# Attention block on one Trainium2 core: the output projection's rows 8 to 11 move from the last stage into the attention loop's fill

## The chip, the cores and the metric

The kernel runs on one NeuronCore of one Trainium2 chip. A core has five instruction streams that run side by side and wait for each other through semaphores: TensorE (PE, matrix products; its weight loads are shown as PEld), VectorE (DVE), ScalarE (ACT), GpSimd (POOL) and SyncE (SP), which only issues transfers between memory and the core. Each stream executes its instructions strictly in the order in which the program holds them. The metric is the device time of one execution in microseconds (us), lower is better; the median of several runs counts.

## What is computed

One layer on x of 2048 rows by 1024 columns. x is normalised and projected to q, k, v, a gate, and the two inputs of a recurrent branch. Eight heads of differential attention run causally over 2048 positions, and a gated linear recurrence runs beside them; both results, 1024 columns each, are concatenated and multiplied by w_out (2048 by 1024); the rows are normalised and added to x. Cut to its core:

```
qh = q.reshape(B, S, 8, 2, 64);  kh = k.reshape(B, S, 8, 2, 64);  vh = v.reshape(B, S, 8, 128)
o = diff_attention(qh, kh, vh, lam)        # softmax(q0 k0) v - lam * softmax(q1 k1) v, causal
y_attn = (rmsnorm(o, subln_g) * (1.0 - lam_init)).reshape(B, S, 1024) * silu(g_attn)
y_lru  = rg_lru(causal_depthwise_conv(x_lru, conv_w, conv_b), ...) * silu(g_lru)
y = jnp.concatenate([y_attn, y_lru], axis=-1) @ w_out
x = x + rmsnorm(y, post_norm_g)
```

All of it is float32. The kernel writes a float32 operand as a high part and a low part of a narrower type and forms each product from three matmuls (high by high, low by high, high by low).

## The kernel before

The sequence is cut into four chunks of 512 positions (j = 0 to 3) and sixteen rows of 128 positions ("row i" below is such a tile, i = 0 to 15). After the input projections, attention runs in two halves: half A takes the query pairs of chunks 0 and 1, half B those of chunks 2 and 3. This case is about half B and what follows it.

**A slot.** `attention` has one slot per unit: a unit is a head, a pair of query tiles (`pr`, 4 to 7 in half B), one of its two tiles and one of the two softmax maps, so half B has U = 128 units (0 to 127) and 12 slots more that only drain. In a slot the scores of the next unit are multiplied (`s`, four PSUM buffers), VectorE takes their maximum (`nm` is its negative, the last step of a unit), ScalarE takes the exponentials, VectorE combines the two maps into weights `p`, PE transposes them (`pw`), ScalarE and VectorE split them (`wh`, `wl`), and PE multiplies them by the values (`o`). Some slots after a chunk's last values a head's result is normalised in six steps, `norm1` to `norm6`: a square on ScalarE, a product with ones on PE (`pm`), an inverse square root on VectorE (`f`), its store and reload in another layout (`r_s`, then `rb`), a product on GpSimd (`yt`), and the store into `ya_s[j]`, from which the output projection reads. Rows 8 to 11 need `ya_s[2]` of all eight heads: the last head stores it at slot 129. Rows 12 to 15 need `ya_s[3]`, stored at slot 137.

**The fill.** Between these pieces stand matmuls of other work, drawn one by one from a generator. In half B it is `fill_out`, the output projection, in groups of 24 matmuls (8 blocks of 128 by three terms) for one row and one half of the output columns (`nh` 0 left, 1 right). The input side r = 1 is the recurrent branch, r = 0 attention. The groups are: r = 1 left and right for all 16 rows, r = 0 left and right for rows 0 to 7, and r = 0 right for row 8: 49 groups. A group loads its row's y (`yraw`, a single buffer, 512 KB), which GpSimd splits in four parts into `yh` and `yl` (two buffers) while the group ahead runs; its sum is in a single PSUM buffer `f`. For r = 0 VectorE adds the partial sum of r = 1 (`part`). When a row has both its halves, `finish` squares it on ScalarE (`junk`), multiplies by the norm's gain on GpSimd, forms the inverse square root on VectorE (`ss`), adds x (`xt`) and stores the output row.

**What sets the order.** The program hands out per slot a budget of fill matmuls (`FB` = 8.25, drawn as `owed`), and places scores, transposes, fill and values by a small clock of its own; the tile framework then orders each engine's stream by its own estimates, and adds the semaphores. SyncE's stream holds all transfers, and each waits there for its own condition with everything behind it.

**The last stage.** A pool of new buffers is opened on the left side of the memory. The remaining r = 0 products are the right halves of rows 9 to 15 and the left halves of rows 8 to 15 (`ps_y`, six PSUM buffers). The left weights (`w3h`, `w3l`) are loaded through SyncE and split on VectorE, three at a time between the right halves.

## Time and profile before

| what | value |
|---|---|
| median of 3 runs (lowest to highest) | 2247.93 us (2242.29 to 2249.29) |
| the profiled execution: its time | 2245.1 us |
| the profiled execution: span from the first to the last instruction | 2243.2 us |
| mean granted TensorE clock | 0.987 of full speed |
| busy share: PE, DVE, ACT, POOL | 96%, 67%, 45%, 36% |
| PE and DVE busy, 1720 to 1902 us (182 us of half B's loop) | 176.8 and 151.2 us |

Times in the views are counted from the span's start. A row of the table of stretches gives, for each engine, its busy time within the stretch and in brackets its instructions, then the granted clock, the busy share of the DMA engines and the bytes moved per second. A row of waits says which engine and line waited for which, in total, how often, and the longest. A row of the groups of instructions gives the count, busy time, mean duration in ns, and the idle time of that engine just before them with what ended most of it. A row of the chain of waits, which is followed back from the last instruction, gives start, duration and what ran or was awaited. "L1073" is line 1073 of the kernel.

### The profile page before, as it was taken

What the parts mean: (1) busy time and instruction counts of PE and PEld (TensorE: products, weight loads), DVE (VectorE), ACT (ScalarE), POOL (GpSimd) and SP (SyncE); (2) the same over time, 40 slices, a digit from 0 to 9 for tenths busy, and PEclk for the clock granted to TensorE, in tenths of its full rate; (3) what the DMA queues carried; (4) which work ended last, traced back from release to release, by engine and by line L of the source; (5) the groups of instructions that cost most, each with busy time, mean ns of one, the idle gap of its engine ahead of it and who ended that gap; (6) DMA issues with size and microseconds to landing.
All of it is one profiled execution on the core that took longest, in us unless ns stands there. A gap on an engine that the chain in (4) does not pass through costs nothing. (4 is left out here: it accounts for less than half of the span.)

```text
span 2243.2 us, 31726 instructions
## 1 busy us (share of the span) xinstructions
PE 2149.8 (96%) x11025; PEld 1786.9 (80%) x11025; DVE 1505.0 (67%) x3296; ACT 1003.3 (45%) x2259; POOL 803.1 (36%) x741
## 2 busy tenths in 40 slices
PE   7999999999899999999999998999999999999888
PEld 7888888888688888788888776888888887888666
DVE  6531144556677767777437776888888888889775
ACT  4211133444544444444225655665656656566211
POOL 1223044434411111111265653233533335345542
PEclk9999999999999999999999998999999999999999
DMA  6554332332478666665452207455464465654573
GB/s 214 151 155 150 103 102 78 97 104 77 117 195 218 165 172 169 175 168 133 132 182 70 67 33 178 117 150 143 124 177 127 124 168 140 169 160 142 161 230 131
DMA packets 346497, 317.93 MB, mean 142 GB/s; under 512 B 20257, under 2 KB 278370, under 8 KB 346338
## 3 DMA queue, kind: packets, MB, share of 16 engines
q1 hardware_dynamic: 346338, 315.91, 50.5%
q8 instruction: 87, 1.43, 0.3%
q14 instruction: 72, 0.59, 0.1%
HBM read 221.41 MB, written 94.44 MB: 141 GB/s over the span
## 5 line engine op out<-in xcount | busy, mean ns | idle before, releaser
L227 PE MATMUL ps<-hh,whi 128*128 128x512 f32 (+1 forms) x1456 | 563.7, 387 | 0.0
L227 PE MATMUL ps<-hh,wlo 128*128 128x512 f32 (+1 forms) x1456 | 562.9, 387 | 0.0
L227 PE MATMUL ps<-hl,whi 128*128 128x512 f32 (+1 forms) x1456 | 561.5, 386 | 0.0
L480 ACT ACTIVATE p<-s,nm 128x512 f32<-128x512 f32 (+3 forms) x640 | 392.6, 623 | 325.4 <-DVE nm L464 284.3
L199 POOL TENSOR_TENSOR wlo<-wraw,whi 128x1024 fp32r<-128x1024 f32 x88 | 221.8, 2521 | 526.4 <-DVE whi L198 173.4
L441 PE MATMUL s<-ks,qs 128*128 128x512 f32 (+2 forms) x1280 | 370.5, 387 | 19.3 <-ACT p L480 15.5
L227 PEld LDWEIGHTS ps<-hl,whi 128*128 128x128 f32 x1456 | 275.3, 189 | 51.7
L457 DVE TENSOR_REDUCE mx<-s 128x1 f32<-128x512 f32 x384 | 257.8, 684 | 87.4 <-PE s L441 86.1
L227 PEld LDWEIGHTS ps<-hh,wlo 128*128 128x128 f32 x1456 | 275.2, 189 | 51.5
L227 PEld LDWEIGHTS ps<-hh,whi 128*128 128x128 f32 x1456 | 275.3, 189 | 50.5
L441 PEld LDWEIGHTS s<-ks,qs 128*128 128x128 f32 x1280 | 213.2, 191 | 76.6 <-ACT p L480 46.6
L516 ACT ACTIVATE wh<-pw 128x512 fp32r<-128x512 f32 (+1 forms) x288 | 160.3, 577 | 158.5 <-PE pw L512 155.3
L70 POOL TENSOR_SCALAR yh<-yraw 128x256 fp32r<-128x256 f32 x196 | 92.6, 491 | 354.5 <-PE f L1073 303.4
L535 PE MATMUL o<-wh,vs 128*128 128x256 f32 (+1 forms) x1152 | 217.9, 280 | 0.2 <-ACT wh L516 0.2
L535 PEld LDWEIGHTS o<-wh,vs 128*128 128x128 f32 x1152 | 192.2, 190 | 17.0 <-ACT wh L516 1.0
L517 DVE TENSOR_TENSOR wl<-pw,wh 128x512 fp32r<-128x512 f32 (+1 forms) x288 | 185.7, 654 | 29.2 <-ACT wh L516 27.4
L498 DVE SCALAR_TENSOR_TENSOR p<-p,rr,p 128x128 f32<-128x128 f32 (+15 forms) x128 | 188.3, 1471 | 3.0
L512 PE MATMUL pw<-ident,p 128*128 128x128 f32 x1088 | 171.7, 273 | 9.9 <-DVE wl L517 5.7
L1073 PE MATMUL f<-woh,yh 128*128 128x512 f32 x392 | 162.3, 414 | 12.6 <-DVE yv L1089 4.6
L512 PEld LDWEIGHTS pw<-ident,p 128*128 128x128 f32 x1088 | 133.7, 140 | 43.6 <-issue 9.4
L535 PE MATMUL o<-wl,vs 128*128 128x256 f32 x576 | 162.8, 283 | 5.2 <-DVE wl L517 4.8
L71 POOL TENSOR_TENSOR yl<-yraw,yh 128x256 fp32r<-128x256 f32 x196 | 162.6, 850 | 0.1
(165 smaller groups left out, 3278.7 us busy)
## 6 DMA issues: line engine op xcount, KB each, us to landing
wraw<-in_w_in_dram SPq DMA_DIRECT2D x96, 512.0 KB, 4.3
qs<-q_s SPq DMA_DIRECT2D x128, 256.0 KB, 4.7
ks<-k_s SPq DMA_DIRECT2D x96, 256.0 KB, 5.6
vs<-v_s SPq DMA_DIRECT2D x48, 512.0 KB, 5.6
xt<-in_x_dram SPq DMA_DIRECT2D x32, 512.0 KB, 4.4
k_s<-hilo SPq DMA_DIRECT2D x64, 256.0 KB, 3.4
q_s<-hilo SPq DMA_DIRECT2D x64, 256.0 KB, 3.4
v_s<-hilo SPq DMA_DIRECT2D x32, 512.0 KB, 4.3
```

What stands on the lines that cost most here:

```text
L71: nc.gpsimd.tensor_tensor(out=lo, in0=src, in1=hi.bitcast(F32), op=ALU.subtract)
L199: nc.gpsimd.tensor_tensor(out=lo, in0=src, in1=hi.bitcast(F32), op=ALU.subtract)
L227: nc.tensor.matmul(out=ps[:, t0:t0 + n], lhsT=a[:, k, :], rhs=b[:, k, t0:t0 + n], start=(k == 0 and m == 0), stop=(k == KC - 1 and m == 2),)
L441: nc.tensor.matmul(out=ps[:, b0 - c0:b0 - c0 + nk], lhsT=qq[:, c, t * P:(t + 1) * P], rhs=kst[h, b0 // CH][:, c, 0:nk], start=(m == 0), st ...
L457: nc.vector.tensor_reduce(out=mx[:, pi:pi + 1], in_=s, axis=AX.X, op=ALU.max)
L480: nc.scalar.activation(out=p[:, c0:c1], in_=sc.pop((u, pi))[:, 0:c1 - c0], func=AF.Exp, bias=negm[u], accum_out=acc,)
L498: nc.vector.scalar_tensor_tensor(out=p0[:, 0:n], in0=p1[:, 0:n], scalar=rr[:, 1:2], in1=p0[:, 0:n], op0=ALU.mult, op1=ALU.add,)
L512: nc.tensor.transpose(pw[:, i * P:(i + 1) * P], wts[h, pr, t][:, kb * P:(kb + 1) * P], ident)
L516: nc.scalar.activation(out=wh[:, 0:n], in_=pw[:, 0:n], func=AF.Copy)
L517: nc.vector.tensor_tensor(out=wl[:, 0:n], in0=pw[:, 0:n], in1=wh[:, 0:n].bitcast(F32), op=ALU.subtract,)
L535: nc.tensor.matmul(out=po[h, j][:, oo:oo + w1 - w0], lhsT=a[:, kb % 4, :], rhs=w[:, w0:w1], start=(kb == 0 and m == 0), stop=(kb == 2 * pr ...
L1073: nc.tensor.matmul(out=ps, lhsT=a[:, k, :], rhs=b, start=(k == 0 and m == 0), stop=(k == 7 and m == 2),)
```

## The change

Five things change. First, r = 0 right for rows 9, 10 and 11 joins the fill, behind row 8: 52 groups. These four rows add the partial sum and store the result back over it (`part_s[1][i]`), and the last stage loads it from there. Second, the budget per slot is 9.4 up to slot 127 and 3 for the eight slots behind it; the fill of rows 8 to 11 may not be loaded before the last head has stored its chunk (`ya_done`), and until then the fill yields nothing, while its budget adds up. Third, in slots from U on, the budget is spent after the slot's transposes and values (this holds for half A as well). Fourth, the finished row of the fill (`yv`) gets a pool of its own with two buffers. Fifth, the last stage's pool moves to the right side, where the attention's buffers were; all eight left weights are loaded first, through ScalarE's queue, and split by ScalarE and VectorE; the order is the right halves of rows 12 to 15, then the left halves of 12, 8, 13, 9, 14, 10, 15, 11, each with its finish, and the loads of a row's y and sum stand ahead of it.

```diff
+    ya_done = set()
...
         def norm6(h, j):
             nc.sync.dma_start(out=ya_s[j][:, h, :], in_=nrm.pop((h, j))[1])
+            ya_done.add((h, j))
...
-            owed += per_slot(s)
-            nf = int(owed)
+            owed += per_slot(s) if s < U + 8 else 0
+            nf = int(owed) if s < U else 0
+            tail_fill = int(owed) if s >= U else 0
...
                     r = next(fill, "end")
                     if r == "end":
                         nf = 0
+                    elif r == "wait":
+                        nf = 0
...
+            for _ in range(tail_fill):
+                r = next(fill, "end")
+                if r in ("end", "wait"):
+                    break
+                owed -= 1
             run("C", combine)
...
-            gen = attention(range(4, 8), kv_p, pools, 4 * CH // SP, lambda s: FB if s > 1 else 6, 6, 5, 1)
+            gen = attention(range(4, 8), kv_p, pools, 4 * CH // SP, lambda s: (9.4 if s > 1 else 6) if s < 128 else 3, 6, 5, 1)
...
-        groups = [(r, nh, i) for r, nh in wsets for i in range((8, 16)[r])] + [(0, 1, 8)]
+        v_p = pb.enter_context(tc.tile_pool(name="rowB", bufs=2, side="right"))
+        groups = [(r, nh, i) for r, nh in wsets for i in range((8, 16)[r])] + [(0, 1, i) for i in range(8, 12)]
...
             for g, (r, nh, i) in enumerate(groups):
+                if ysp is None:
+                    while (H - 1, i // 4) not in ya_done:
+                        yield "wait"
+                    ysp, parts = load_y(r, i)
+                    for p in parts:
+                        split(*p)
...
-                if nxt:
+                ysp, parts = None, ()
+                if nxt and (nxt[0] or nxt[2] < 8 or (H - 1, nxt[2] // 4) in ya_done):
                     ysp, parts = load_y(*nxt[::2])
...
-                        yv = f_p.tile([P, D], F32, tag="yv", name="yv", bufs=1)
+                    if nh and i < 8:
+                        yv = v_p.tile([P, D], F32, tag="yv", name="yv")
...
-                    ends[i] = finish(f_p, i, yv, 1, 1, nc.gpsimd if i < FE else nc.vector)
-                    if i < 8:
-                        ends.pop(i)()
+                    finish(f_p, i, yv, 1, 1, nc.gpsimd)()
...
-                        nc.sync.dma_start(out=part_s[0][i][:, 0:CH], in_=st)
+                        nc.sync.dma_start(
+                            out=part_s[1][i][:, CH:] if i >= 8 else part_s[0][i][:, 0:CH], in_=st,
+                        )
...
-        y_p = p3.enter_context(tc.tile_pool(name="y", bufs=2))
+        y_p = p3.enter_context(tc.tile_pool(name="y", bufs=2, side="right"))
...
-            yh = y_p.tile([P, 8, P], F32R, tag="yh3", name="yh3", bufs=6)
+            yh = y_p.tile([P, 8, P], F32R, tag="yh3", name="yh3", bufs=5)
...
+        def load_w0(k):
+            raw = y_p.tile([P, CH], F32, tag="woraw3", name="woraw3", bufs=8)
+            nc.scalar.dma_start(out=raw, in_=w_out2[k * P:(k + 1) * P, 0:CH])
+            return raw
...
+            nc.scalar.activation(out=hi, in_=raw, func=AF.Copy)
+            nc.vector.tensor_tensor(out=lo, in0=raw, in1=hi.bitcast(F32), op=ALU.subtract)
...
         def left(i):
+            ends[i] = finish(y_p, i, yvs[i], 2, 1 + (i == 11), nc.gpsimd)
             ps = out_mm(i, w0)
...
-        load_ya(9)
-        load_ya(10)
-        for i in range(9, 12):
...
+        raws = [load_w0(k) for k in range(8)]
+        for k, raw in enumerate(raws):
+            split_w0(k, raw)
+        load_ya(12)
+        load_ya(13)
+        begin(12)
+        begin(13)
+        for i in range(12, 16):
+            if i < 14:
+                load_ya(i + 2)
+                begin(i + 2)
+            elif i == 14:
+                load_ya(8)
+                begin(8)
             right(i)
...
+        for i in range(8, 12):
+            left(i + 4)
+            if i < 11:
+                load_ya(i + 1)
+                begin(i + 1)
             left(i)
```

How the instructions move, at three places. **PE at the end of the loop:** the scores of the last unit (`s`), with the values (`o`) and transposes (`pw`) between them and what follows. Before:

```order
L441 MATMUL s<-ks,qs 128x512 x2
L535 MATMUL o<-wl,vs 128x256
L535 MATMUL o<-wh,vs 128x256
L441 MATMUL s<-ks,qs 128x512 x2
L535 MATMUL o<-wh,vs 128x256
L535 MATMUL o<-wl,vs 128x256
L557 MATMUL pm<-ones_235,sq 128x2 x4
L1073 MATMUL f<-wol_20001,yh 128x512
L1073 MATMUL f<-woh_20011,yh 128x512
L1073 MATMUL f<-woh_20011,yl 128x512
L1073 MATMUL f<-wol_20012,yh 128x512
L1073 MATMUL f<-woh_20070,yh 128x512
```

Now (the product with ones, `pm`, is the norm of the last head's chunk 2; it stood behind the last scores before):

```order
L559 MATMUL pm<-ones_235,sq 128x2 x4
L537 MATMUL o<-wl,vs 128x256
L443 MATMUL s<-ks,qs 128x512 x2
L537 MATMUL o<-wh,vs 128x256
L514 MATMUL pw<-ident,p_20689 128x128
L443 MATMUL s<-ks,qs 128x512 x2
L514 MATMUL pw<-ident,p_20834 128x128
L443 MATMUL s<-ks,qs 128x512 x2
L514 MATMUL pw<-ident,p_20689 128x128
L514 MATMUL pw<-ident,p_20834 128x128
L443 MATMUL s<-ks,qs 128x512 x2
L514 MATMUL pw<-ident,p_20689 128x128
```

The fill (`f`) that followed the last scores is gone there; none stands between the scores of unit 124 and the place that follows, and all groups up to 47 stand ahead of unit 124's.

**PE in the drain, now:** the last transposes, the first matmuls of group 48 (row 8) and a value between them:

```order
L537 MATMUL o<-wl,vs 128x256
L514 MATMUL pw<-ident,p_20967 128x128
L514 MATMUL pw<-ident,p_21069 128x128
L514 MATMUL pw<-ident,p_20967 128x128
L514 MATMUL pw<-ident,p_21069 128x128
L514 MATMUL pw<-ident,p_20967 128x128
L514 MATMUL pw<-ident,p_21069 128x128 x2
L1087 MATMUL f<-woh_19208,yh 128x512
L537 MATMUL o<-wh,vs 128x256
L1087 MATMUL f<-woh_19208,yl 128x512
L1087 MATMUL f<-wol_19209,yh 128x512
L1087 MATMUL f<-woh_19217,yh 128x512
```

Group 48 begins behind the last transposes; one row of the last values stands behind its first matmul, the others behind its last.

**SyncE in the drain, now:** the transfers of the last head's norm (`r_s`, `rb`, `ya_s`), of groups 48 to 51 (`yraw` the load of y, `part` the sum to be added, `fo` the result) and of row 12 (the last row here). The first piece ends with the load for group 51:

```order
L572 DMA r_s_2_194<-f_21135 128x4
L576 DMA rb<-r_s_2_194 128x512
L585 DMA ya_s_198<-yt 128x512
L992 DMA yraw<-ya_s_198 128x8x128 x2
L1109 DMA part_s_8_220<-fo 128x512
L992 DMA yraw<-ya_s_198 128x8x128
L1083 DMA part<-part_s_9_221 128x512
L992 DMA yraw<-ya_s_198 128x8x128
```

and it goes on:

```order
L1109 DMA part_s_9_221<-fo 128x512
L1083 DMA part<-part_s_10_222 128x512
L1109 DMA part_s_10_222<-fo 128x512
L572 DMA r_s_3_195<-f_21471 128x4
L1083 DMA part<-part_s_11_223 128x512
L576 DMA rb<-r_s_3_195 128x512
L585 DMA ya_s_199<-yt 128x512
L1109 DMA part_s_11_223<-fo 128x512
L1130 DMA yraw_21595<-ya_s_199 128x8x128
```

Before, the loads of rows 9 to 11 for the last stage stood between the norm of chunk 3 and row 12's load; now groups 49 to 51 are loaded ahead of that norm's `r_s`, and row 12's load stands behind the store of group 51's result.

More of the change, by code (lines that the diff above doesn't have):

```diff
@@ L1058, in fill_out @@
                 c0 = nh * CH
-                if i >= 8 and r == 0:
-                    yv = f_p.tile([P, D], F32, tag="yv", name="yv", bufs=1)
-                    nc.sync.dma_start(out=yv, in_=part_s[1][i])
-                    part = yv[:, CH:]
-                    ys[i], yvs[i] = ysp, yv
-                elif r == 0:
-                    if nh:
-                        yv = f_p.tile([P, D], F32, tag="yv", name="yv", bufs=1)
+                if r == 0:
+                    if nh and i < 8:
+                        yv = v_p.tile([P, D], F32, tag="yv", name="yv")
                         nc.sync.dma_start(out=yv[:, 0:CH], in_=part_s[0][i][:, 0:CH])
@@ L1085, in fill_out @@
                             raw_wo(*nxt[:2], k + 4)
-                    if k % 2 and nxt:
+                    if k % 2 and parts:
                         split(*parts[k // 2])
-                if r == 0 and nh == 1:
+                if r == 0 and nh == 1 and i < 8:
                     nc.vector.tensor_tensor(out=yv[:, CH:], in0=ps, in1=part, op=ALU.add)
-                    ends[i] = finish(f_p, i, yv, 1, 1, nc.gpsimd if i < FE else nc.vector)
-                    if i < 8:
-                        ends.pop(i)()
+                    finish(f_p, i, yv, 1, 1, nc.gpsimd)()
                 else:
@@ L1116, in load_ya @@
             nc.sync.dma_start(out=raw, in_=ya_s[i // 4][:, :, (i % 4) * P:(i % 4 + 1) * P])
-            yh = y_p.tile([P, 8, P], F32R, tag="yh3", name="yh3", bufs=6)
-            yl = y_p.tile([P, 8, P], F32R, tag="yl3", name="yl3", bufs=6)
+            yh = y_p.tile([P, 8, P], F32R, tag="yh3", name="yh3", bufs=5)
+            yl = y_p.tile([P, 8, P], F32R, tag="yl3", name="yl3", bufs=5)
             split3(yh, yl, raw, SY)
@@ L1134, in hymba_kernel, with split_w0, begin, right @@
         w0 = []
-        def right(i):
+        def load_w0(k):
+            raw = y_p.tile([P, CH], F32, tag="woraw3", name="woraw3", bufs=8)
+            nc.scalar.dma_start(out=raw, in_=w_out2[k * P:(k + 1) * P, 0:CH])
+            return raw
+        def split_w0(k, raw):
+            hi = y_p.tile([P, CH], F32R, name=f"w3h{k}", bufs=1)
+            lo = y_p.tile([P, CH], F32R, name=f"w3l{k}", bufs=1)
+            nc.scalar.activation(out=hi, in_=raw, func=AF.Copy)
+            nc.vector.tensor_tensor(out=lo, in0=raw, in1=hi.bitcast(F32), op=ALU.subtract)
+            w0.append((hi, lo))
+        def begin(i):
             yvs[i] = y_p.tile([P, D], F32, tag="yv3", name="yv3", bufs=5)
             nc.sync.dma_start(out=yvs[i], in_=part_s[1][i])
+        def right(i):
             ps = out_mm(i, w1)
             nc.vector.tensor_tensor(out=yvs[i][:, CH:], in0=ps, in1=yvs[i][:, CH:], op=ALU.add)
-            ends[i] = finish(y_p, i, yvs[i], 2, 1 + (i == 15), nc.vector if FY else nc.gpsimd)
         def left(i):
+            ends[i] = finish(y_p, i, yvs[i], 2, 1 + (i == 11), nc.gpsimd)
             ps = out_mm(i, w0)
@@ L1146, in left @@
             ends.pop(i)()
-        load_ya(9)
-        load_ya(10)
-        for i in range(9, 12):
-            for k in ((0, 1, 2), (3, 4, 5), (6, 7))[i - 9]:
-                raw = y_p.tile([P, CH], F32, tag="woraw3", name="woraw3")
-                nc.sync.dma_start(out=raw, in_=w_out2[k * P:(k + 1) * P, 0:CH])
-                hi = y_p.tile([P, CH], F32R, name=f"w3h{k}", bufs=1)
-                lo = y_p.tile([P, CH], F32R, name=f"w3l{k}", bufs=1)
-                split3(hi, lo, raw, SW)
-                w0.append((hi, lo))
-            right(i)
-            load_ya(i + 2)
-        for i in range(8, 16):
+        raws = [load_w0(k) for k in range(8)]
[12 more added lines that the diff above has]
+                begin(8)
+            right(i)
+        for i in range(8, 12):
[3 more added lines that the diff above has]
+                begin(i + 1)
             left(i)
-            if i < 12:
-                right(i + 4)
-                if i + 6 < 16:
-                    load_ya(i + 6)
     pf.close()
```

## The prediction

> **What bounds the kernel now.** First the page, then a table of the last stretches, then what TensorE (PE) waited for in them.
>
> ```profile
> span 2243.2 us, 31726 instructions
> PE 2149.8 (96%) x11025; PEld 1786.9 (80%) x11025; DVE 1505.0 (67%) x3296; ACT 1003.3 (45%) x2259; POOL 803.1 (36%) x741
> ```
>
> PE is the bound by share, so only its idle time can be won or lost: the change moves matmuls and adds none. Where that idle time lies, by stretches (us, then busy us of each engine):
>
> ```profile
> core 0: us, PE busy (x) PEld busy (x) DVE busy (x) ACT busy (x) POOL busy (x), PEclk, DMA share, GB/s
> 1946.00:2060.00 114.00, 111.44 (x652) 94.22 (x651) 100.74 (x240) 71.57 (x195) 60.23 (x71) 1.00 0.51 143
> 2060.00:2081.00 21.00, 20.14 (x117) 17.20 (x117) 20.29 (x48) 12.21 (x34) 8.06 (x10) 1.00 0.32 100
> 2081.00:2112.00 31.00, 26.28 (x170) 22.43 (x168) 22.73 (x53) 11.64 (x28) 18.58 (x24) 0.99 0.51 154
> 2112.00:2172.00 60.00, 46.18 (x169) 35.22 (x170) 43.24 (x73) 7.24 (x20) 32.55 (x29) 0.89 0.75 241
> 2172.00:2234.50 62.50, 62.45 (x264) 50.25 (x262) 36.67 (x92) 7.96 (x22) 17.71 (x12) 0.97 0.42 144
> 2234.50:2243.20 8.70, 0.00 (x0) 0.00 (x0) 4.14 (x13) 0.72 (x2) 1.26 (x1) 0.70 0.30 121
> ```
>
> In the score loop PE is nearly full, but in its last 21 us VectorE (DVE) is just as full (20.29). The drain (2081 to 2112) and the hand-over to the last stage (2112 to 2172) hold 18.5 us of idle PE, at a lowered clock. The maxima of the last scores, which end the loop:
>
> ```profile
> L464 DVE TENSOR_REDUCE nm<-mx x4: 142/151/157, 2059.9 to 2080.8; 128x1 f32<-128x4 f32 x4
> ```
>
> So unit 124's maximum stands at 2060 and unit 127's, the last (call it T), at 2081. From 2060 to the end PE waited most for:
>
> ```profile
> PE f L1073 <- DVE yv L1089: 4.6, 1, 4.6
> PE ps_y L1128 <- DVE yh L202: 4.5, 1, 4.5
> PE f L1073 <- DVE f L563: 1.9, 1, 1.9
> ```
>
> The first is a row's finish blocking VectorE, the second is row 12's load behind other loads. Both places are rewritten.
>
> **The loop, denser.** By the order of instructions 1019 fill matmuls stood ahead of unit 124's last score, now 1152: 133 more. The chain of waits and the waits of the loop (1374 to 2060) price them:
>
> ```profile
> 2070.40 1.16 PE f L1073 x5
> ...
> PE s L441 <- ACT p L480: 11.0, 16, 1.9
> ```
>
> 1.16/5 is 0.232 us each: 133 are +30.9 us. Against it, waits of scores for ScalarE's exponentials (11.0 us in 16 pieces) can be filled by work that stands between; bounds 0 and -11, I take -3, because the scores stay where a free buffer puts them and few of the waits have fill left in their slot.
>
> All eight row finishes now fall into the loop; before, most fell into its end and the drain. One finish on VectorE:
>
> ```profile
> L1006 DVE SCALAR_TENSOR_TENSOR xt<-yv,ss,xt 128x1024 f32<-128x1024 f32 x5 | 6.4, 1281 | 2.3 <-DMA xt<-in_x_dram 2.1
> L96 DVE TENSOR_SCALAR ss<-ss 128x1 f32<-128x1 f32 x15 | 4.0, 266 | 0.2
> L97 DVE SCALAR_TENSOR_TENSOR ss<-ss 128x1 f32<-128x1 f32 x15 | 2.6, 171 | 0.1
> L1002 DVE TENSOR_TENSOR ss<-ss 128x1 f32<-128x1 f32 x5 | 1.3, 260 | 4.6 <-ACT junk L995 4.6
> L89 DVE TENSOR_SCALAR ss<-ss 128x1 int32<-128x1 int32 x5 | 0.8, 154 | 0.1
> ```
>
> 1.28 + 3 x 0.27 + 3 x 0.17 + 0.26 + three small ones of about 0.15 are 3.3 us. In 1946 to 2060 stood two chains and one xt; by the new order of VectorE seven finishes stand ahead of unit 124's end. That is 5 x 3.3 + 1.3 = 17.8 more, so 118.5 us of VectorE; at the 97% that it reached in the next row (20.29 of 21) it needs 122.4. PE with 13 more matmuls there needs 111.44 + 3.0 + its 2.6 of idle = 117. The stretch turns to VectorE: +5 (0 if the second row buffer smooths it, +10 if every finish stalls VectorE by its 1.4 us of idle, 4.6 and 2.1 over five). Unit 124: 2060 + 30.9 - 3 + 5 = 2092.9.
>
> **The end of the loop, empty.** Between units 124 and 127 there is no fill now (about 32 matmuls in the old order). VectorE there:
>
> ```profile
> L1006 DVE SCALAR_TENSOR_TENSOR xt<-yv,ss,xt 128x1024 f32<-128x1024 f32 x2 | 2.6, 1278 | 0.0
> L96 DVE TENSOR_SCALAR ss<-ss 128x1 f32<-128x1 f32 x4 | 1.0, 259 | 0.0
> L97 DVE SCALAR_TENSOR_TENSOR ss<-ss 128x1 f32<-128x1 f32 x4 | 0.6, 146 | 0.0
> ```
>
> These and one add (0.7) leave, 4.9, and one finish (3.3) stays: 18.7 of VectorE, at 97% 19 us instead of 21. PE's 20.14 - 7.4 does not bind. T = 2112.
>
> **Group 48 waits for row 8.** Its y comes from the last head's norm, which ends in slot 129; what ran there before was rows 4 to 7, whose y had long been there. The links (chain of waits; times to landing; the loads from issue to landing):
>
> ```profile
> 2087.52 2.56 DMA r_s<-f
> ...
> 2090.16 6.14 DMA rb<-r_s
> ...
> 2096.44 2.63 POOL yt L580
> ...
> DMA to landing us min/median/max: 3.5/4.1/6.1
> ...
> ya_s<-yt SPq DMA_DIRECT2D x4, 256.0 KB, 2.0
> r_s<-f SPq DMA_DIRECT2D x3, 2.0 KB, 2.1
> part<-part_s SPq DMA_DIRECT2D x9, 256.0 KB, 4.2
> ...
> DMA to landing us min/median/max: 4.0/4.8/7.6
> ...
> L580 POOL TENSOR_TENSOR yt<-yt,rb x16: 1521/1549/2641, 1458.4 to 2127.9; 128x512 f32<-128x512 f32 x16
> ```
>
> The first landing row is rb's, the second yraw's. In the new order the reciprocal root stands right behind T with nothing but one other instruction: 3.5 us (6.5 before: T to 2087.5). Then r_s 2.1, rb 4.1, the product 1.6, the store 2.0, yraw 4.8 and gaps: yraw lands at T + 18.3 (25 at the times of the chain above, 15.5 at the minima). Call this L: 2130. PE has only transposes and values until then; after them it stands at group 48's first matmul, with the last 24 values behind that.
>
> **Four groups on one raw buffer.** GpSimd splits each y in four parts:
>
> ```profile
> 2099.04 0.78 POOL L70 TENSOR_SCALAR yh<-yraw 128x256 fp32r<-128x256 f32 x2
> 2099.77 1.44 POOL L71 TENSOR_TENSOR yl<-yraw,yh 128x256 fp32r<-128x256 f32 x2
> ```
>
> Twice this, 4.35 us, and only then the single raw buffer takes the next row: 4.35 + 4.8 = 9.1 per group, while its matmuls need 24 x 0.232 = 5.6. In the loop a group lasted 2.6 slots and hid it; here the load is bare. Group 51's y is split at L + 32. Worse is SyncE's order: group 51's load waits there for the split of group 50 (L + 22.6); behind it stand the store of group 49, part of row 10 (4.2, so L + 27.5), the store of group 50 and only then r_s of rows 12 to 15 at about L + 28.2.
>
> **Row 12.** From there the same links: 2.1 + 4.1 + 1.6 + 2.0 + 4.8 and, for the last stage's split:
>
> ```profile
> 2147.87 6.90 DMA yraw<-ya_s
> ...
> 2154.79 0.69 DVE yh L202
> ...
> L203 POOL TENSOR_TENSOR yl<-yraw,yh 128x1024 fp32r<-128x1024 f32 x5 | 12.3, 2468 | 9.9 <-DVE yh L202 9.9
> ...
> 2171.69 62.78 PE ps_y L1128 x264
> ```
>
> 0.7 + 2.5, with gaps 18.3: row 12 runs from L + 46.5 (40 at minima, 53 at the slow times). Before, the right halves of rows 9 to 11 covered this; now PE is idle from about L + 33. Then 288 matmuls without a stop at 62.78/264 = 0.238: 68.5, and after so long a gap a slow start:
>
> ```profile
> 2132.24 0.76 PE L1073 MATMUL f<-woh,yh 128*128 128x512 f32 x1 [4.59 <-DVE yv L1089]
> ...
> 2135.67 0.40 PE L1073 MATMUL f<-wol,yh 128*128 128x512 f32 x1
> ```
>
> Eight matmuls took 3.4 us instead of 1.9, so +1. The end after the last matmul stays 8.7 (last row of the table).
>
> **The left weights.** Eight loads on ScalarE's queue stand behind its last square, about L + 23; their split is done long before left needs it at L + 69. What leaves is PE's wait for these weights in the hand-over, one part of its idle 18.5 us, already out of my sum. Their 2.1 MB meet group 51's load and rb; at the 241 GB/s of the table they are 8.7 us of traffic. I take 0, since group 51 is not what row 12 waits for; bound +4.
> The Trainium skill (DMA: Bandwidth & Descriptors, Issuing engines are not separate DMA queues) says that transfers started by ScalarE and SyncE run on the same 16 engines and interleave, so that another queue saves issue time alone. By that rule the +4 is the likelier end, and the sum would be 2259 instead of 2255; no run here has a second queue.
>
> **The rest.** The first half's drain is reordered too (fill behind transposes), but its fill has two accumulators and no load to wait for: 0, bounds -2 and +2. The second row buffer, the other side of the memory and five instead of six split buffers are in the terms above or free of PE.
>
> **Sum:** 2130 + 46.5 + 68.5 + 1 + 8.7 = 2254.7 of span; the profiled execution took 2245.1, 1.9 over its span, so 2256.6, say 2257, +0.5%. The median of the runs is 2.8 above the profiled one, within their spread.
>
> **Rivals.** *The loop swallows the fill* (faster): all 11 us of score waits are filled, VectorE keeps up (no +5), and links run at their minima. Unit 124 2079.9, T 2099, L 2114.5, end 2114.5 + 40 + 78.2 = 2232.7, time 2235. For it: PE has those waits and the drain's DMA engines are quieter than before. Against: VectorE's 20.29 of 21. *Loop free, drain as forecast* (no change): -5 and 0 in place of -3 and +5: 2247.7, time 2250. For it: yv waits disappear with two buffers. *Collisions in the drain* (slower still): rb, yraw and part run at the times of the chain while the left weights load; L at T + 22, row 12 at L + 53: 2265, time 2267. It decides once rb takes 6 us instead of 4.1. *The fill is not moved as said*: the order rules it out; only its wait for row 8 can differ.
>
> **How the numbers follow.** Forecast 0.49 (its own range 2250 to 2264), swallowed 0.18, loop free 0.20, collisions 0.13. About 0.3% (7 us) is the least that a measurement of this kernel tells from no change: from 2241 to 2255. Faster 0.18; same: loop free and the low end of the forecast, 0.27; slower 0.55. Range 2237 to 2269.
>
> **What would show it.** Right: no fill between units 124 and 127, that stretch at 18 to 20 us; unit 124 near 2093; a PE gap ahead of group 48 released by GpSimd's yh or yl; groups 48 to 51 about 9 us apart, each released by GpSimd; a gap of 10 us or more ahead of the first last-stage matmul, released by VectorE's cast or GpSimd's yl behind yraw; then 288 matmuls without a gap. Wrong: unit 124 before 2083, group 48 within 12 us of T, or row 12 within 5 us of group 51's end.

## The result and the profile after

The changed kernel takes 2268.61 us (median of 4 runs, 2266.16 to 2271.08), the kernel before, run beside it, 2245.47. The ratio is 1.0102, with a 95% interval of 1.0078 to 1.0126: slower by 1.0%. Forecast were 2257 us (+0.5%), within 2237 to 2269. The profiled execution of the changed kernel took 2271.1 us, 1.8 over its span.

First the head of the page, then the table of stretches, cut at the places that the prediction named (columns as before).

```profile
span 2269.3 us, 31770 instructions
PE 2153.8 (95%) x11025; PEld 1793.3 (79%) x11025; DVE 1491.8 (66%) x3287; ACT 1006.0 (44%) x2267; POOL 803.5 (35%) x768
```

```profile
1968.00:2095.30 127.30, 117.26 (x669) 95.77 (x667) 120.38 (x300) 74.59 (x211) 55.24 (x67) 1.00 0.57 166
2095.30:2115.40 20.10, 15.24 (x85) 12.22 (x85) 18.62 (x46) 12.02 (x31) 0.67 (x1) 0.92 0.06 26
2115.40:2131.20 15.80, 12.33 (x75) 10.74 (x74) 9.31 (x23) 7.60 (x17) 1.97 (x3) 0.78 0.25 68
2131.20:2164.00 32.80, 25.17 (x109) 20.22 (x110) 8.00 (x17) 0.73 (x2) 16.69 (x31) 0.90 0.29 89
2164.00:2182.20 18.20, 6.97 (x22) 4.92 (x21) 1.39 (x2) 0.00 (x0) 3.88 (x2) 0.69 0.67 185
2182.20:2257.00 74.80, 68.54 (x287) 55.68 (x287) 51.16 (x95) 14.45 (x38) 33.53 (x21) 0.93 0.61 200
2257.00:2269.30 12.30, 0.00 (x0) 0.00 (x0) 7.73 (x22) 0.86 (x4) 3.34 (x3) 0.50 0.39 136
```

PE's work is the same 11025 matmuls. Its idle time lies in the loop's end, in the drain, and behind the last matmul. The maxima of units 124 to 127 in the view of one tile, which give unit 124 at 2095.3 and T at 2115.4:

```profile
L466 DVE TENSOR_REDUCE nm<-mx x4: 142/148/155, 2095.2 to 2115.3; 128x1 f32<-128x4 f32 x4
```

**Groups 48 to 51.** From PE's timeline, the first matmuls of groups 48, 49 and 50, the last of the values (`o`) that stand between them, and the last matmul of group 50; in brackets the idle time ahead and what ended it.

```profile
2131.23 0.51 PE L1087 MATMUL f<-woh,yh 128*128 128x512 f32 x1 [0.59 <-POOL yh L70]
...
2139.67 0.50 PE L1087 MATMUL f<-woh,yh 128*128 128x512 f32 x1 [0.94 <-POOL yh L70]
...
2149.24 0.47 PE L1087 MATMUL f<-woh,yh 128*128 128x512 f32 x1 [2.06 <-DVE fo L1108]
...
2154.04 0.28 PE L537 MATMUL o<-wl,vs 128*128 128x128 f32 x1
...
2157.89 0.40 PE L1087 MATMUL f<-wol,yh 128*128 128x512 f32 x1
```

The groups start 8.4 and 9.6 us apart, then 12.7 (group 51 at 2161.89). The last value of the last head is multiplied only at 2154.04, behind groups 48 and 49 and half of 50. Until then ScalarE cannot square that head (2154.41), and the norm of rows 12 to 15 cannot begin. Its inverse square root on VectorE (timeline; first, slowest and last step) ends at 2161.8:

```profile
2156.58 0.16 DVE L565 SCALAR_TENSOR_TENSOR f<-pm,f 128x4 f32<-128x4 f32 x1 [0.79 <-PE pm L559]
...
2157.44 0.68 DVE L81 SCALAR_TENSOR_TENSOR f<-f 128x4 f32<-128x4 f32 x1
...
2161.66 0.15 DVE L82 SCALAR_TENSOR_TENSOR f<-f 128x4 f32<-128x4 f32 x1
```

SyncE issues its store `r_s` 0.3 us behind that end, right behind the store of group 50's result (`part_s`, SyncE's timeline):

```profile
2152.11 0.53 SPq L992 DMA_DIRECT2D yraw<-ya_s  x1
...
2161.77 0.32 SPq L1109 DMA_DIRECT2D part_s<-fo  x1
2162.14 0.42 SPq L572 DMA_DIRECT2D r_s<-f  x1
...
2165.68 0.32 SPq L576 DMA_DIRECT2D rb<-r_s  x1
2170.75 0.32 SPq L585 DMA_DIRECT2D ya_s<-yt  x1
```

So the root came last here, but SyncE's queue was close behind it. The addition of group 50's result (`fo`, 0.7 us) stands in the middle of the root. Without the root, that result could have been stored at about 2159, and `r_s` could have followed at about 2159.4, 2.7 us earlier than it did (an estimate from the end of group 50's last matmul and these durations).

PE's waits from 2060 on have row 12's load at their head. Group 51 waits behind the same root, because the addition that empties the sum buffer (`fo` of group 50) stands in it:

```profile
PE ps_y L1142 <- DVE yh L202: 9.5, 1, 9.5
...
PE f L1087 <- DVE f L82: 3.6, 1, 3.6
```

**The last stage.** The chain of waits (start, duration, what ran) passes from PE to VectorE in its middle and never returns:

```profile
2172.81 5.88 DMA yraw<-ya_s
...
2182.17 30.50 PE ps_y L1142 x119
2212.70 0.70 DVE yv L1173
...
2214.18 2.37 DVE ss L1013
...
2220.85 0.70 DVE yv L1173
...
2229.18 0.61 DVE yv L1173
...
2237.24 0.70 DVE yv L1173
...
2243.27 0.61 DVE yv L1173
```

Only 119 of the 288 matmuls are on the chain. From the first left halves on, each row's addition waits for VectorE's finish of the row ahead: 8.2 us apart three times, then 5.9. A row's 24 matmuls need 24 x 0.238 = 5.7. PE is never held up, since six PSUM buffers stand between, but it is done by 2250.7 and the finishes run on to 2269.3: 18.6 us behind the last matmul instead of 8.7. The 8.2 has its reason in the second kind of row, `ss` L1013: an addition of 128x1 that takes 2.37 us there, and 0.16 in the last five rows. GpSimd's timeline stands beside it:

```profile
2214.12 2.40 POOL L203 TENSOR_TENSOR yl<-yraw,yh 128x1024 fp32r<-128x1024 f32 x1 [11.97 <-DVE yh L202]
```

The addition starts 0.06 us behind the split and ends with it. The same pair stands once in the kernel before, where the alternating order kept it off the path (VectorE's and GpSimd's timelines):

```profile
2186.19 2.40 DVE L1002 TENSOR_TENSOR ss<-ss 128x1 f32<-128x1 f32 x1 [0.25 <-ACT junk L995]
```

```profile
2186.17 2.41 POOL L203 TENSOR_TENSOR yl<-yraw,yh 128x1024 fp32r<-128x1024 f32 x1 [3.20 <-DVE yh L202]
```

The 5.9 us of the later rows hold more of the same kind. The change also moved the first half of a finish, the square and the product of the right half, from the right half's place to the left half's, so that two products of GpSimd (2.55 us) now stand beside VectorE's root where one (1.30 us) stood before. The second of the root's steps with two inputs (L97) lasts until GpSimd's second product ends (VectorE's timelines; a late row of the changed kernel, then one of the kernel before):

```profile
2240.47 0.91 DVE L97 SCALAR_TENSOR_TENSOR ss<-ss 128x1 f32<-128x1 f32 x1
```

```profile
2226.61 0.16 DVE L97 SCALAR_TENSOR_TENSOR ss<-ss 128x1 f32<-128x1 f32 x1
```

In the kernel before, the last four left halves follow each other too, without a right half or a split between them, but 5.56 us apart, and VectorE waits 0.27 us for PE ahead of each of the last three: there PE set the pace. No run moves the second product back alone, so its share is not tested.

### The profile page after: what moved, and what is told of

Read it like the earlier page. It is cut to its first block, busy times and chain, and to the rows that moved or that the text cites. A ratio compares the mean times of both kernels' runs of the same rounds, so it can differ in the third digit from the quotient of the medians.

```text
span 2269.3 us, 31770 instructions
## 1 busy us (share of the span) xinstructions
PE 2153.8 (95%) x11025; PEld 1793.3 (79%) x11025; DVE 1491.8 (66%) x3287; ACT 1006.0 (44%) x2267; POOL 803.5 (35%) x768
## 3 DMA queue, kind: packets, MB, share of 16 engines
q10 hardware_dynamic: 1152, 2.10, 0.3%
## 5 line engine op out<-in xcount | busy, mean ns | idle before, releaser
L443 PE MATMUL s<-ks,qs 128*128 128x512 f32 (+2 forms) x1280 | 365.7, 386 | 25.6 <-ACT p L482 22.4
L70 POOL TENSOR_SCALAR yh<-yraw 128x256 fp32r<-128x256 f32 x208 | 99.4, 496 | 370.9 <-PE f L1087 327.0
L1087 PE MATMUL f<-woh,yh 128*128 128x512 f32 x416 | 170.0, 409 | 14.5 <-ACT fo L1113 6.9
L1087 PE MATMUL f<-woh,yl 128*128 128x512 f32 x416 | 169.8, 408 | 1.0 <-POOL yl L71 1.0
L1087 PE MATMUL f<-wol,yh 128*128 128x512 f32 x416 | 169.0, 406 | 0.0
```

The source lines that it names most:

```text
L70: nc.gpsimd.tensor_scalar(out=hi, in0=src, scalar1=1.0, scalar2=1.0, op0=ALU.mult, op1=ALU.mult)
L443: nc.tensor.matmul(out=ps[:, b0 - c0:b0 - c0 + nk], lhsT=qq[:, c, t * P:(t + 1) * P], rhs=kst[h, b0 // CH][:, c, 0:nk], start=(m == 0), st ...
L1087: nc.tensor.matmul(out=ps, lhsT=a[:, k, :], rhs=b, start=(k == 0 and m == 0), stop=(k == 7 and m == 2),)
```

## The experiments

Ratios are to the kernel before, run beside each on the same chip; the changed kernel has 1.0102. "Alternating" is the last stage in the order right 12, left 8, right 13, left 9, right 14, left 10, right 15, left 11, and then the left halves of 12 to 15, as follows (the last row's finish is halved at row 15 instead of 11):

```diff
         load_ya(12)
-        load_ya(13)
+        load_ya(8)
         begin(12)
-        begin(13)
-        for i in range(12, 16):
...
+        begin(8)
+        for k in range(4):
+            right(12 + k)
+            if k < 3:
+                load_ya(13 + k)
+                begin(13 + k)
+            left(8 + k)
+            if k < 3:
+                load_ya(9 + k)
+                begin(9 + k)
+        for i in range(12, 16):
+            left(i)
```

### The budget back at 8.25

```diff
-lambda s: (9.4 if s > 1 else 6) if s < 128 else 3
+lambda s: (8.25 if s > 1 else 6) if s < 128 else 3
```

> The changed kernel with the old budget of 8.25 fill matmuls per slot in place of 9.4; all else as changed. Theory (the drain is bound by one raw buffer, 9.1 us per group, and by the wait for row 8): about 109 matmuls move from the loop into the drain, so the last score maximum comes 25 to 30 us earlier (about 2088), but groups 44 to 51 then go through the single raw buffer one after another, 8 x 9 us, and the time stays within 2256 to 2268 (2268.6 now). Rival (the denser loop itself, where VectorE cannot follow, is what was lost): the drain stays as long as now from the last score on, and the time falls to 2240 to 2250.

Measured: 2264.74, ratio 1.0073 [1.0054, 1.0092]. T is back at 2085.3, but 192 matmuls of fill now stand behind T instead of 96, with five row finishes among them, and PE waits there (waits of 2085 to 2200):

```profile
PE f L1087 <- POOL yh L70: 10.6, 2, 6.8
PE f L1087 <- DVE fo L1108: 9.1, 2, 6.5
```

The time hardly falls: what is taken out of the loop is paid again behind it. How much of the loss lies in the loop with 9.4 shows only beside 8.75, below.

### One finished-row buffer, and the pool on the other side

```diff
-        v_p = pb.enter_context(tc.tile_pool(name="rowB", bufs=2, side="right"))
+        v_p = pb.enter_context(tc.tile_pool(name="rowB", bufs=1, side="right"))
```

> The changed kernel with one buffer instead of two for the fill's finished row. Theory: the second buffer bought little, because the loop is bound by VectorE's work and not by waits for the row: 2266 to 2271. Rival (two buffers kept VectorE from stalling in every finish, 1.4 us each): 2274 to 2282.

Measured: 2266.67, ratio 1.0075 [1.0049, 1.01]; the interval overlaps that of the changed kernel. The second row buffer carries nothing that can be measured here.

```diff
-        y_p = p3.enter_context(tc.tile_pool(name="y", bufs=2, side="right"))
+        y_p = p3.enter_context(tc.tile_pool(name="y", bufs=2))
```

> The changed kernel with the last stage's pool on the left side of the memory, as before the change. Theory (on the right the left weights' buffers lie where the attention's last product lay, so ScalarE's loads start only when that product is stored and collide with row 12's load): the eight loads start about 18 us earlier, next to ScalarE's last square, row 12's load lands in 4.8 instead of 5.9 us and the sums of the last stage in 4 to 5 instead of 7.7: time 2265 to 2268. Rival (the collision holds up the whole last stage): 2255 to 2262.

Measured: 2267.51, ratio 1.0087 [1.0065, 1.0109], no difference. The expectation that the eight loads of the left weights would start 18 us earlier failed: ScalarE's queue issues them at 2170.91 here and, in the changed kernel, at

```profile
2172.92 10.85 ACTq L1152 DMA_DIRECT2D woraw<-in_w_out_dram  x8
```

ScalarE's last instruction ahead of them is the square at 2154.41. In both runs the loads go out 2.2 us behind the issue of the last chunk's store (`ya_s`, 2168.72 here and 2170.75 there; it lands 2.0 us after its issue) and 0.1 us behind row 12's own load. With the budget 8.75 alone (below) the store is issued at 2129.59 and the loads at 2131.83, again 2.2 us later, but 4.3 us ahead of row 12's load. So they go with that store, as the expectation said, but on either side of the memory. Why they wait for it on the left side too was not found.

### The alternating last stage

The diff is the one above.

> The changed kernel with another order of the last stage: right 12, left 8, right 13, left 9, right 14, left 10, right 15, left 11, then left 12 to 15, instead of all right halves first. Theory (left halves in a row are bound by VectorE's finish, 5.9 to 8.2 us each against 5.6 us of matmuls): rows finish during the right halves, the stretch from the first last-stage matmul to the end falls from 87 us to 78 to 82 (up to 3 us may be lost on left weights that come late), time 2260 to 2264. Rival (the last stage is slow because of the lowered clock after the gap ahead of it): no change, 2267 to 2270.

Measured: 2260.69, ratio 1.0053 [1.0033, 1.0073], about 8 to 11 us less than the changed kernel. In the profiles 6 us of this lie in the last stage: from row 12's first running matmul to the end it takes 81 us instead of 87. The rest lies ahead of it, where the two kernels are alike: T is 2110.6 in this profile, 2115.4 in that of the changed kernel, and between 2110.6 and 2117.8 in all runs with 9.4. With a right half between two left halves VectorE has 11.2 us for a finish, and PE sets the pace; only the last four left halves, with nothing between them, are 5.95 us apart again. The 2.4 us addition still occurs, once:

```profile
L1013 DVE TENSOR_TENSOR ss<-ss x8: 145/160/2401, 2193.5 to 2248.6; 128x1 f32<-128x1 f32 x8
```

### Two raw buffers for the fill's y

With one finished-row buffer, since the memory does not hold both.

```diff
-YR = 1
+YR = 2
...
-        v_p = pb.enter_context(tc.tile_pool(name="rowB", bufs=2, side="right"))
+        v_p = pb.enter_context(tc.tile_pool(name="rowB", bufs=1, side="right"))
```

> The changed kernel with two raw buffers for the fill's y (and one buffer instead of two for the finished row, which alone made no difference). Theory (groups 48 to 51 are paced by load, then split, 8.5 us each, and SyncE holds r_s of rows 12 to 15 behind the load for group 51): the groups follow each other in 6 to 7 us, row 12 starts 38 to 43 us after group 48 instead of 48, time 2257 to 2261. Rival (their pace is set by the partial sums and the single sum buffer, and row 12's chain by its own links): no change, 2265 to 2269.

Measured: 2264.48, ratio 1.0068 [1.0044, 1.0091], some 2 us less than with one raw buffer (the run with one finished-row buffer, 1.0075), which the intervals do not tell apart. The groups do run closer. Row 12's first matmul stands 41.6 us behind group 48's, as the theory had it, against 46.5 in the run with one raw buffer and one row buffer and 48.4 in the changed kernel. The time did not follow by as much: T is 1.7 us later in this profile than in that run's, and the gap ahead of row 12, 9.5 us in the changed kernel and 11.5 in that run, is now (waits from 2090 on)

```profile
PE ps_y L1142 <- DVE yh L202: 12.7, 1, 12.7
```

The load for group 51 no longer holds anything: SyncE has issued it by 2142.1, and `r_s` goes out at 2156.9, within 0.4 us of its root's end and again right behind the store of group 50. The root's chain begins with the last values, and here too they stand behind groups 48 and 49: ScalarE squares the last head at 2151.7. GpSimd is idle during the root now, and this takes 2.6 us instead of 5.2 (4.1 with one raw buffer and one row buffer):

```profile
2153.92 0.16 DVE L565 SCALAR_TENSOR_TENSOR f<-pm,f 128x4 f32<-128x4 f32 x1 [0.80 <-PE pm L559]
...
2156.41 0.15 DVE L82 SCALAR_TENSOR_TENSOR f<-f 128x4 f32<-128x4 f32 x1
```

Two raw buffers, one row buffer and the alternating last stage together:

> Two raw buffers (with one buffer for the finished row) and the alternating last stage together, budget 9.4 as changed. Theory: the two gains add up, 8 and 9 us: 2249 to 2254. Rival (row 12's own chain ends at the same time whatever the groups do): 2259 to 2262, as with the alternating order alone.

Measured: 2254.61, ratio 1.0031 [1.0013, 1.005], just over the theory's range and well under the rival's. The interval overlaps that of the alternating order alone, [1.0033, 1.0073].

### All three repairs, with 8.25 and with 8.75

Two raw buffers, one row buffer, alternation, and the budget 8.25:

> As the one before, with the old budget of 8.25: four and a half more groups run in the drain. Theory (with two raw buffers fill in the drain costs its matmuls alone, and rows 4 to 7 cover the wait for row 8): last score maximum at 2085, then 60 us of PE work and few gaps, row 12 ready before the fill ends: 2228 to 2238, faster than the kernel before. Rival (the drain is then bound by the finishes of rows 4 to 7 with single row buffers, about 10 us each): 2243 to 2252.

Measured: 2263.98, ratio 1.0076 [1.006, 1.0091]. My own theory was far off, and even the rival too low. At 8.25 the repairs bring nothing, because the stretch behind T is set by the finishes of rows 3 to 7 and the splits between them (waits of 2085 to 2200):

```profile
PE f L1087 <- DVE yv L1103: 11.7, 3, 5.4
PE f L1087 <- POOL yh L70: 11.0, 2, 10.2
```

The same with the budget 8.75:

> The same with a budget of 8.75: about two groups are left when the scores end, which should just cover the wait for row 8. Theory: 2228 to 2238, at or below the run with 8.25, since fewer finishes stand in the drain. Rival (VectorE is already too full in the loop at this budget): 2240 to 2250, between the runs with 8.25 and 9.4.

Measured: 2232.52 (2229.35 to 2236.57), ratio 0.9937 [0.9917, 0.9958]: faster than both kernels. The stretches behind T:

```profile
2085.80:2117.10 31.30, 27.51 (x177) 22.78 (x175) 25.84 (x67) 12.09 (x29) 11.75 (x16) 1.00 0.46 151
2117.10:2154.10 37.00, 27.07 (x102) 20.97 (x103) 15.59 (x25) 6.75 (x14) 25.60 (x29) 0.91 0.87 272
2154.10:2219.00 64.90, 64.90 (x284) 52.91 (x282) 42.01 (x83) 8.25 (x24) 27.18 (x17) 1.00 0.53 172
2219.00:2233.00 14.00, 0.17 (x1) 0.00 (x0) 8.11 (x24) 2.06 (x6) 3.74 (x3) 0.61 0.41 151
```

144 matmuls of fill stand behind T, and two of their groups need no row 8: they run while that row's load travels (31.3 us with 27.5 of PE). The drain's last values stand among them, ahead of group 48, so that the norm of rows 12 to 15 runs beside the groups instead of behind them.

### Which part of it

With 8.75, and each of the two other parts alone or neither. Neither, which is the changed kernel with 8.75 in place of 9.4:

> The changed kernel with a budget of 8.75 matmuls per slot in place of 9.4, and nothing else. Theory (the wait for row 8's chain is what costs, and with 8.75 the last two or three groups of rows 5 to 7 stand between the last score maximum and group 48 and cover it): first matmul of group 48 at about 2117 without a gap of more than 3 us ahead of it, the reciprocal root of rows 12 to 15 stands behind group 49's load and no longer behind group 51's, so row 12 starts without a gap of 9 us; the groups stay 8 to 10 us apart on one raw buffer (+8) and the last stage stays at 87 us (+6): 2232.5 + 14 = 2246, between 2240 and 2254. Rival (it took the alternating last stage and the second raw buffer, the budget alone moves the same idle time about): 2262 or more.

Measured: 2249.03, ratio 1.0006 [0.9995, 1.0017]. Group 48 starts at 2119.7, behind a gap of 0.9 us. The last value is multiplied 24.5 us behind T, against 38.6 in the changed kernel, and the root's store stands right behind group 49's load (PE's and SyncE's timelines):

```profile
2113.23 0.27 PE L537 MATMUL o<-wl,vs 128*128 128x128 f32 x1
```

```profile
2117.16 0.52 SPq L992 DMA_DIRECT2D yraw<-ya_s  x1
...
2118.55 0.32 SPq L572 DMA_DIRECT2D r_s<-f  x1
```

Row 12's first matmul stands at 2146.6, before group 51. Behind it PE still waits 4.6 us for the split, and 6.0 us ahead of group 49.

The three budgets, with nothing else changed, show where the gain lies. T and the end are those of the profiles. The maxima of units 124 to 127 with 8.75 (the view of one tile) give T = 2088.8:

```profile
L466 DVE TENSOR_REDUCE nm<-mx x4: 140/146/148, 2070.1 to 2088.6; 128x1 f32<-128x4 f32 x4
```

| budget per slot | fill matmuls ahead of T | T | from T to the end |
|---|---|---|---|
| 8.25 | 1056 | 2085.3 | 179.2 |
| 8.75 | 1104 | 2088.8 | 157.6 |
| 9.4 | 1152 | 2115.4 | 153.9 |

A step of 48 matmuls is 11.1 us of PE at 0.232. From 8.25 to 8.75 T moves by only 3.4 us, and the stretch behind it is 21.6 shorter: what 8.25 loses, it loses behind T. From 8.75 to 9.4 T moves by 26.7 us, 15.6 more than the matmuls, and the stretch behind it is only 3.7 shorter. So about two thirds of what 8.75 regains from 9.4 lie in the loop, and one third behind T; in the other runs too T comes at least 21 us later with 9.4 (2110.6 to 2117.8) than with 8.75 (2085.1 to 2088.8). Part of the loop's share can be seen: with 9.4 the last fill ahead of T ends 27 us before it, and units 124 to 127 take 20.1 us with none among them; with 8.75 they take 18.5 us with 24 fill matmuls among them. Where in the loop the rest arises is not shown.

With two raw buffers and one row buffer:

> Budget 8.75, two raw buffers for the fill's y and one finished-row buffer; the last stage in the order of the changed kernel (rights of 12 to 15, then the lefts in a row). Theory (VectorE's chain of finishes sets the last stage, 87 us against 81): 5 to 7 us over the kernel that alternates, 2238, between 2234 and 2243. Rival (the alternation is worth nothing once row 12 comes early): 2232.5 within 2.

Measured: 2242.47, ratio 0.9980 [0.9969, 0.9991], at the upper end of the theory's range.

With the alternating last stage:

> Budget 8.75 and the alternating last stage, with the single raw buffer (and two finished-row buffers) of the changed kernel. Theory (groups 9 us apart instead of 5.6 on one raw buffer, partly covered by row 12's matmuls that may now stand between them): 4 to 12 us over the kernel with two raw buffers, 2240, between 2235 and 2246. Rival (the raw buffer is free of the path as in the changed kernel itself, where the second one brought 2 us): 2232.5 to 2235.

Measured: 2241.97, ratio 0.9979 [0.9967, 0.9992], within the theory's range.

| budget per slot | fill matmuls behind T | as the change | two raw buffers, one row buffer | alternating | both |
|---|---|---|---|---|---|
| 9.4 | 96 | 1.0102 | 1.0068 | 1.0053 | 1.0031 |
| 8.75 | 144 | 1.0006 | 0.9980 | 0.9979 | 0.9937 |
| 8.25 | 192 | 1.0073 | not run | not run | 1.0076 |

Going from 9.4 to 8.75 is worth 0.7 to 1.0% in every column, and it is a valley: at 8.25 most or all of it is lost again. The raw buffers gain 0.2 to 0.4%, the alternation 0.3 to 0.5%; single steps of 0.2% lie within the intervals. Both rivals of the two single parts fell. By the ratios the alternation is worth 9.7 us when row 12 comes early (5 to 7 expected) and the raw buffers 9.4; in the profiles the stretch from T to the end is 5.2 and 5.1 us shorter with both, so part of the difference may be scatter between the runs.

### The low part of y on VectorE

Only in the last stage; `SY` chooses the engine of that split.

```diff
-SY = 0
+SY = 1
```

> The changed kernel with the low part of y in the last stage formed on VectorE instead of GpSimd; nothing else. Theory (the 128x1 add of a finish takes 2.3 us instead of 0.16 because GpSimd works on its 2.4 us split at the same time): the add stays under 0.3 us in every row, three rows that took 8.2 us take about 5.95 + 0.7 for the cast + 1.2 for the split = 7.2 or less, and row 12 starts 1 us earlier: 3 to 5 us less than the changed kernel, 2264 to 2267. Rival (the add waits for something else, ScalarE's sums for one): it keeps its 2.3 us beside 1.2 us more of VectorE per row, and the time is 2271 or more.

Measured: 2261.69, ratio 1.0063 [1.0046, 1.0081], 9 us less than the changed kernel. The theory's pitch came out (7.3 us three times instead of 8.2; 7.2 expected), but the addition did not fall to 0.3 us. In the three rows it takes 1.26 (VectorE's timeline; L86 is a step with one input), and GpSimd's product of the same finish, which is two instructions of 1.27 in the later rows, stands beside it and is itself longer, 3.44 for the two:

```profile
2208.32 1.23 DVE L203 TENSOR_TENSOR yl<-yraw,yh 128x1024 fp32r<-128x1024 f32 x1
2209.46 1.26 DVE L1013 TENSOR_TENSOR ss<-ss 128x1 f32<-128x1 f32 x1
2210.75 0.15 DVE L86 TENSOR_SCALAR ss<-ss 128x1 f32<-128x1 f32 x1
```

```profile
2208.52 3.44 POOL L1007 TENSOR_TENSOR yv<-yv,pgt 128x512 f32<-128x512 f32 x2 [17.19 <-ACT junk L1006]
```

The addition's length follows GpSimd's instruction beside it: 2.4 with the split of 128x1024, 1.26 with the product of 128x512, 0.16 with none running yet. Three rows at 0.9 us account for 2.7 us of the gain, and row 12's second matmul, which waits for the split, comes 1.3 us sooner behind its first: 4.0 together, within the 3 to 5 that were expected. The rest lies where the edit does nothing. T is 1.9 us earlier in this profile, and row 12's first matmul, which needs only the cast, is 2.7 us closer to T; in the runs with the alternating order and with the pool on the left, which do not touch that stretch either, it is closer by 2.9 and 3.3. So the 9 us are not all the edit's, and its interval just overlaps that of the changed kernel.

## Why the prediction was right, and which terms were not

The direction was right and the time within the range, but only just: 2268.6 against an upper end of 2269. The forecast of 2257 was 12 us short, the time lies outside of the 2250 to 2264 that the forecast gave itself, and the largest miss, the end behind the last matmul, stands in no rival. That the range holds is in part luck. The prediction's sum against the profile after, term by term (T and L were rounded in it, so that the terms add up to 2254.9):

| term | predicted | measured | difference |
|---|---|---|---|
| unit 124's maximum | 2092.9 | 2095.3 | +2.4 |
| units 124 to 127 | 19 | 20.1 | +1.1 |
| T to L (row 8's y landed, PE at group 48) | 18.3 | 15.8 | -2.5 |
| L to row 12 running | 46.5 | 51.0 | +4.5 |
| 288 matmuls, with the slow start | 69.5 | 68.5 | -1.0 |
| after the last matmul | 8.7 | 18.6 | +9.9 |
| span | 2254.7 | 2269.3 | +14.6 |

**The loop, denser: right.** Unit 124 was to come 32.9 us later than before (30.9 for the matmuls, -3, +5); it came 35.3 later. The 3 us that I took off for filled waits failed in sign. The waits of scores for ScalarE grew from 11.0 to 17.9 us (PE's waits of 1374 to 2095):

```profile
PE s L443 <- ACT p L482: 17.9, 18, 2.7
```

ScalarE in turn waits for VectorE's maxima, and VectorE is busy for 120.4 of the last 127.3 us, PE for 117.3: in line with the term of +5. What neither the sum nor a rival saw is how steep the cost is here: with 8.75, 48 matmuls fewer, T comes 26.7 us earlier.

**The end of the loop, empty: right.** No fill, 20.1 us, VectorE 18.6 busy (18.7 forecast). The prediction books this as 2 us saved; but with 8.75 the same four units take 18.5 us and carry 24 fill matmuls besides.

**Group 48 waits for row 8: right in kind.** The links came a little under my durations (y from T in 15.8 us). The gap ahead of group 48 is small, 0.6 us released by GpSimd's `yh`: transposes and values filled 12.3 of the 15.8 us.

**Four groups on one raw buffer: right for two, wrong in its meaning.** Two pitches of 8.4 and 9.6 against 9.1, released by GpSimd; the third group waited for VectorE. But the reason that I gave for the late norm of rows 12 to 15, the store behind other work in SyncE's queue, was only one of two. `r_s` was issued at L + 31 (L + 28.2 forecast), within 0.4 us of its root's end. The queue would have let it go at about L + 28; the root came later. What was late there was PE: the prediction says that group 48's first matmul has "the last 24 values behind that", and never asks when these run. They ran by L + 23, spread behind three groups that wait for loads, and the root hung on them. Two raw buffers brought row 12 to 41.6 us behind group 48, but only some 2 us in time, within the intervals. The budget of 8.75 brought about 21 (ratios 1.0102 and 1.0006), about a third of it behind T. It puts two free groups into the wait and the values ahead of group 48, and with them `r_s` ahead of group 50's store in SyncE's queue, so no run separates the values from the queue.

**Row 12: right.** A gap of 9.5 us released by VectorE's cast and 1.8 by GpSimd's split (10 or more forecast). Its load took 5.88 us instead of 4.8.

**The last stage: the term that failed.** "The end after the last matmul stays 8.7" carried the row of the old order into the new one. The prediction counts VectorE's finish as 3.3 us of busy time in the loop, but never lays it out as a chain beside 5.7 us of matmuls. With its addition, the squares that it waits for and the steps between, it is 5.9 us from row to row, and 8.2 with the split beside it. This is 9.9 of the 14.6 us. The row of the old order did not carry over for a second reason: there the chain kept PE's pace of 5.56 us, with one of GpSimd's products beside it instead of two. The alternating order took 6 us off, and in 9.4 as in 8.75 it pays in every pair of the table.

The Trainium skill (SBUF — State Buffer, Who interferes with whom) states that a VectorE instruction with two inputs in the memory of the core contends with a GpSimd instruction that reads it, that the ports which the two share are an exclusive lock, and that the order of issue decides who blocks. The trace agrees: the addition with two inputs, issued 0.06 us behind the split, goes from 0.16 to 2.37 us and ends with it, and the steps with one input in the same finish (L86, L96) keep their 0.15 and 0.27. By that rule the left halves with a split beside their finish were the dear ones from the start; the prediction did not weigh it.

**The left weights.** The prediction had their loads at about L + 23; they were issued at 2172.9, L + 42, behind the last chunk's store and with row 12's load. The weights were still in time for the first left half. The +4 of the bound was not seen apart: at most the 1.1 us by which row 12's load was longer. The rule on queues that the prediction weighed is that of the Trainium skill (DMA: Bandwidth & Descriptors, Issuing engines are not separate DMA queues): transfers of both engines interleave. The trace agrees in kind, not in size: the three loads of sums (`yv`) that SyncE issued beside the eight took 11.3 us to land (median), against 4.3 in the kernel before. No wait of PE behind 2183 shows them.

**The half-A drain and the second row buffer**, at 0: right. The first maximum of half B stands at 1374.1 us before and at 1374.2 after, and one row buffer measures the same as two.

**The rivals.** "The loop swallows the fill" and "Loop free" fell with unit 124 at 2095. "Collisions in the drain" has the nearest number, 2267, but not its mechanism: it needed `rb` at 6 us and L at T + 22, and the profile has row 8 at T + 15.8.

## What to carry to other kernels

Do not let independent work run out before the loop that it fills, and keep some of it for the wait behind the loop (here 48 matmuls, neither 0 nor 96). When both a loop and the drain behind it change, take the time up to the end of the loop and the time behind it apart before a cause is named. Work that needs a late result should not stand ahead of work that the next late result needs; that this was the cause here is argued, not separated. When an order is changed, lay out the off-path engine's work of one step as a chain, with its waits, against the bound engine's time for that step; a share of 68% busy (51 of 75 us) said nothing, since the chain was 5.9 against 5.7 us. And a tiny instruction with a large duration in the groups of instructions is a question to ask of the engine beside it.

## What the runs showed of the hardware

An addition of 128x1 with two inputs on VectorE lasts as long as the GpSimd instruction that started just before it (2.4, 1.26, or 0.16 us alone), and the inverse square root on 128x4 goes from 2.6 to 5.2 us when GpSimd splits beside it (an addition of 0.7 us stands in both). The hold works both ways: GpSimd's two products went from 2.55 to 3.44 us beside VectorE's split. ScalarE's queue needed 10.85 us to issue eight loads of 256 KB while row 12's load and two sums were under way.
